# Two score products at a time: 64-row second products in the two halves of TensorE's rows

## The chip, the core and the metric

The kernel runs on one core of one Trainium2 chip. The metric is device time in microseconds (us) of one execution. All times below come from the times of three runs of the kernel before and from one profiled execution of it.

## The reference, cut to what matters

One transformer block on 2048 tokens of width 1024, in float32. Its input projection feeds two kinds of attention, and a gated convolutional feed-forward layer (1024 to 2 x 2816 and back) follows. Two of the score products matter here.

```python
# dense ("a"): 4 heads, each with 2 components c of 64 features; softmax per component, then a difference
logits = jnp.einsum('bthcd,bshcd->bhcts', qb, k).astype(jnp.float32) * scale
...
p = jax.nn.softmax(logits, axis=-1)
attn = p[:, :, 0] - lam * p[:, :, 1]
return jnp.einsum('bhts,bshe->bthe', attn.astype(v.dtype), v)

# selection: 8 index heads of 64 features against one shared key; the 256 best keys of each query stay
s_h = jax.nn.relu(jnp.einsum('bthd,bsd->bths', iqb, ik).astype(jnp.float32))
score = jnp.einsum('bth,bths->bts', iwb.astype(jnp.float32), s_h)
score = jnp.where(causal[None], score, -jnp.inf)
_, idx = lax.top_k(score, topk)
```

The sparse attention ("b", 8 heads) then works on the selected keys alone. Both attentions are causal, over 16 blocks of 128 queries.

## The kernel before

**Split operands.** Every float32 operand of a large product is kept as a float16 pair, a high part and a low part, and a product is the sum of three: high by high, high by low, low by high. A query or key of 64 features fills only half of TensorE's 128 rows, so the two halves hold different parts. In the dense logits a component's query is held twice (both halves the same, a tile of high parts and a tile of low parts), and its key has the high part in one half and the low part in the other: component 0 has its high part in rows 0 to 63, component 1 in rows 64 to 127. One product of the query's high part over 128 rows (L962) gives two of the three terms, and a second one of its low part (L963) gives the third and, unasked for, low by low. In the selection it is the query that has high and low parts in the two halves (even heads high in rows 0 to 63, odd heads in rows 64 to 127), and the key is held twice, as a tile of high parts (L1042) and one of low parts (L1043).

**The dense unit.** `a_units` yields one `a_unit` for each of 4 heads and 16 query blocks, so 64 in all. Block i has n = 128 (i + 1) keys, in chunks of up to 512. Stage `s1` goes through component 0 and then component 1: for each chunk two matmuls into a PSUM bank of tag "s", and `logits`, in which VectorE moves the chunk to the SBUF tile `big`, adds the bias near the diagonal and takes a maximum (L905, L908, L910). After the last chunk of a component come a tiny VectorE operation on the maxima (L967) and ScalarE's Exp over all n keys with a running sum (L968). Stage `s2` begins with a reciprocal of the second sum (L973), joins the two components (L977), splits the result and issues transposing DMAs (`pT`). Stage `s3` multiplies with the values (L989, L990). `pipeline` runs `s3` of one unit, `s2` of the next and `s1` of the one after side by side.

**The selection.** `att_i` takes two query blocks at a time. For each chunk of 512 keys and each of 8 heads it makes two matmuls into a bank of tag "si"; for head 0 VectorE takes the bank at once (L1046), for the other seven ScalarE makes the ReLU (L1050) and VectorE adds it to the score (L1051). Then a bitwise search for the threshold follows, 31 rounds of counting (L1073 on VectorE, L1089 on ScalarE).

**Banks.** `PSB` gives PSUM's eight banks: during the first two blocks `mm` 2, `tp` 1, `s` 2, `si` 2, `o` 1, later `mm` 2, `s` 3, `si` 2, `o` 1. The sparse units and some transposes use "s" too.

**Order.** Every engine works through its instructions in the order in which the program emits them. `timeline` picks that order: each part (selection I, dense A, sparse B and C, feed-forward F and O) is a generator that yields its own estimate of time, and the part whose due time is earliest goes on to its next yield. So between two yields of the selection or the dense logits, matmuls of the output projection or the feed-forward layer (`acc3`, L402 to L404) are usually placed. The yields of the two loops that change are

```python
yield (c1 - c0) / 960 + 0.15        # dense logits, per component and chunk
yield (c1 - c0) / 960 + 0.1         # selection, per head and chunk
```

Of the kernel before, what the change touches and what calls it, by code (L numbers as in the profile page):

```python
# [22 lines left out]
P = 128  # L23
# [58 lines left out]
def block_kernel(ctx: ExitStack, tc, x, c, w_ada, b_ada, g_attn, w_in, q_norm_a, k_norm_a, q_norm_b, k_norm_b,  # L82
# [3 lines left out]
    V, S, G, PE = nc.vector, nc.scalar, nc.gpsimd, nc.tensor  # L86
# [23 lines left out]
    def stiny(name, n=1, dt=F32):  # L110
        return small.tile([P, n], dt, name=name)
# [294 lines left out]
    def split(hi, lo, src, scale):  # L406

        S.activation(hi, src, AF.Copy, scale=scale)  # L408
        V.scalar_tensor_tensor(lo, src, scale, hi, op0=ALU.mult, op1=ALU.subtract)  # L409
# [451 lines left out]
    def chunks(n):  # L861
        out_, c0 = [], 0
        while c0 < n:
            out_.append((c0, min(n, c0 + 512)))
            c0 += 512
        return out_

    def s_ps(w, tag="s"):
        return psum.tile([P, 512], F32, name=tag, tag=tag, bufs=PSB[tag])[:, :w]
# [3 lines left out]
    def big(n):  # L873

        w = 512 if n <= 512 else 1024 if n <= 1024 else T
        at = part["at"] if part.get("w") == w else XW
        if at == XW:
            part.update(w=w, at=0, tile=X.tile([P, XW], F32, name="big", tag="big", bufs=BUFS["big"]))
            at = 0
        part["at"] = at + w  # L880
        return part["tile"][:, at:at + w]
# [9 lines left out]
    def q_tile(name, src, tag="q"):  # L891
        q = X.tile([P, 8 if tag == "qi" else 4, P], F16, name=name, tag=tag, bufs=BUFS[tag])
        n = src.shape[1] // P
        nc.sync.dma_start(q[:, 0:n].rearrange("p h q -> p (h q)"), src)
        return q

    def logits(ps, l, c0, c1, n, near, far, mx, nm):

        f = min(c1, max(c0, n - 256))
        for a0, a1 in ((c0, f), (f, c1)):  # L900
            if a1 <= a0:
                continue
            src, acc = ps[:, a0 - c0:a1 - c0], mx[:, nm:nm + 1]
            if a0 >= n - 256:
                V.tensor_tensor_reduce(l[:, a0:a1], src, near[:, 256 - (n - a0):256 - (n - a1)], 1.0, -3e38,  # L905
                                       op0=ALU.add, op1=ALU.max, accum_out=acc)
            elif far is None:
                V.tensor_scalar(l[:, a0:a1], src, 1.0, None, op0=ALU.mult, op1=ALU.max, accum_out=acc)  # L908
            else:
                V.tensor_tensor_reduce(l[:, a0:a1], src, far[:, a0:a1], 1.0, -3e38, op0=ALU.add, op1=ALU.max,  # L910
                                       accum_out=acc)
            nm += 1
        return nm
# [15 lines left out]
    def weights_v(d, pv):  # L929

        for t_ in d["pT"]:
            pv(*t_)
            yield 0.1
# [13 lines left out]
    def a_unit(t, h, i, first, ks, vs, nb, out_, os_):  # L947
        n = (i + 1) * P
        d = {}

        def s1():
            qt = q_tile("qa", qa_s[i][:, h * 512:(h + 1) * 512])
            d["L"], d["sum"] = [], stiny("a_sum", 2)
            for cc in range(2):
                l = big(n)
                d["L"].append(l)
                mx = stiny("a_mx", 5)
                nm = 0
                for c0, c1 in chunks(n):
                    ps = s_ps(c1 - c0)  # L960
                    rhs = ks[c0 // 512][:, 0:(c1 - c0) // P, cc * P:(cc + 1) * P]
                    PE.matmul(ps, qt[:, 2 * cc], rhs, start=True, stop=False)  # L962
                    PE.matmul(ps, qt[:, 2 * cc + 1], rhs, start=False, stop=True)  # L963
                    nm = logits(ps, l, c0, c1, n, nb, None, mx, nm)
                    yield (c1 - c0) / 960 + 0.15
                m = stiny("a_m")
                V.tensor_scalar(mx[:, :nm], mx[:, :nm], ga_neg, None, op0=ALU.mult, op1=ALU.min, accum_out=m)  # L967
                S.activation(l[:, :n], l[:, :n], AF.Exp, scale=ga_inv, bias=m, accum_out=d["sum"][:, cc:cc + 1])  # L968

        def s2():  # L970
            L, ssum = d["L"], d["sum"]
            bt = stiny("a_bt")
            V.reciprocal(bt, ssum[:, 1:2])  # L973
            V.tensor_scalar(bt, bt, ssum[:, 0:1], nlam, op0=ALU.mult, op1=ALU.mult)
            for c0 in range(0, n, 1024):
                c1 = min(n, c0 + 1024)
                V.scalar_tensor_tensor(L[0][:, c0:c1], L[1][:, c0:c1], bt, L[0][:, c0:c1], op0=ALU.mult, op1=ALU.add)  # L977
            yield n / 960
            yield from weights_t(d, i, L[0], gam)

        def s3():
            ssum = d["sum"]
            po = s_ps(512, "o")

            def pv(pp, b0, b1):
                for j in range(b0, b1):
                    v = vs[j // 4][:, j % 4]
                    hi, lo = pp[:, j - b0], pp[:, b1 - 2 * b0 + j]
                    PE.matmul(po[:, 0:256], hi, v, start=(j == 0), stop=False)  # L989
                    PE.matmul(po[:, 0:128], lo, v[:, 0:128], start=False, stop=(j == i))  # L990

            yield from weights_v(d, pv)
            o = X.tile([P, 2, P], F32, name="oa", bufs=2)
            S.activation(o[:, 1], po[:, 128:256], AF.Copy)
            V.tensor_tensor(o[:, 0], po[:, 0:128], o[:, 1], op=ALU.add)
            ss = stiny("a_ss", 4)
            S.activation(o[:, 1], o[:, 0], AF.Square, accum_out=ss[:, 0:1])
            V.tensor_scalar(ss[:, 1:2], ssum[:, 0:1], ssum[:, 0:1], eps_o, op0=ALU.mult, op1=ALU.mult)
            V.scalar_tensor_tensor(ss[:, 2:3], ss[:, 0:1], 1.0 / 128, ss[:, 1:2], op0=ALU.mult, op1=ALU.add)  # L999
            G.tensor_tensor(ss[:, 3:4], ss[:, 2:3], mhalf[:, 0:1], op=ALU.pow)  # L1000
            V.tensor_scalar(out_, o[:, 0], ss[:, 3:4], None, op0=ALU.mult)

        def s4():
            n_ = i - first + 1
            pt = s_ps(n_ * P)
            for j in range(n_):
                PE.transpose(pt[:, j * P:(j + 1) * P], os_[:, j], idf)
            ot = X.tile([P, 2, 2, P], F16, name="ota", bufs=1)
            pt = pt.rearrange("p (b q) -> p b q", q=P)
            split(ot[:, :, 0], ot[:, :, 1], pt, sub_c)  # L1010
            nc.sync.dma_start(ot_s[t][:, h, first % 4:first % 4 + n_], ot)
            yield 0.5

        return [s1(), s2(), s3()] if first is None else [s1(), s2(), s3(), s4()]
# [3 lines left out]
    def att_i(b0, nb_):  # L1018

        t = b0 // 4  # L1020
        for b1 in range(max(b0, 2), b0 + nb_, 2):
# [8 lines left out]
            for c in range(t + 1):  # L1030
                ki = X.tile([P, 4, 256], F16, name="ki", bufs=BUFS["ki"])
                nc.sync.dma_start(ki, ki_s[c])
                for j, i in enumerate(blks):
                    n = (i + 1) * P
                    sc_, qi = scs[j], qis[j]
                    c0, c1 = c * 512, min(c * 512 + 512, n)
                    if c1 <= c0:
                        continue
                    kk = ki[:, 0:(c1 - c0) // P]
                    for h in range(8):  # L1040
                        ps = s_ps(c1 - c0, "si")
                        PE.matmul(ps, qi[:, h], kk[:, :, 0:P], start=True, stop=False)  # L1042
                        PE.matmul(ps, qi[:, h], kk[:, :, P:2 * P], start=False, stop=True)  # L1043
                        w = iw_all[:, i, h:h + 1]
                        if h == 0:
                            V.tensor_scalar(sc_[:, c0:c1], ps, 0.0, w, op0=ALU.max, op1=ALU.mult)  # L1046
                        else:
                            nr += 1
                            r = rl[:, nr % 2, :c1 - c0]
                            S.activation(r, ps, AF.Relu)  # L1050
                            V.scalar_tensor_tensor(sc_[:, c0:c1], r, w, sc_[:, c0:c1], op0=ALU.mult,  # L1051
                                                   op1=ALU.add)
                        yield (c1 - c0) / 960 + 0.1
                    if c1 == n:
                        V.tensor_tensor(sc_[:, n - P:n], sc_[:, n - P:n], cmask, op=ALU.add)
                    V.tensor_copy(mks[j][:, c0:c1], sc_.bitcast(BF16).rearrange("p (n t) -> p n t", t=2)[:, c0:c1, 1])
# [57 lines left out]
            for j, i in enumerate(blks):  # L1114
                n = ns[j]
# [250 lines left out]
    with tc.tile_pool(name="early", bufs=1) as pool:  # L1366
        with tc.tile_pool(name="psum1", bufs=1, space=PSUM) as psum, tc.tile_pool(name="early2", bufs=1) as pool2:
# [40 lines left out]
            rs = rest()  # L1408
# [81 lines left out]
```

## Time and profile before

| | |
|---|---|
| time, median of 3 runs | 3229.09 us (3227.54 to 3232.38) |
| time of the profiled execution | 3229.96 us |
| its span, first to last instruction | 3228.3 us |
| busy: TensorE (PE) | 2823.8 us, 87% |
| busy: VectorE (DVE) | 2543.7 us, 79% |
| busy: ScalarE (ACT) | 2008.1 us, 62% |
| busy: GpSimd (POOL) | 1227.3 us, 38% |
| mean granted TensorE clock | 0.951 of full speed |

The profile has a line for each instruction: when it started and how long it is put down for. PE is a matmul, PEld the load of its weights. Matmuls overlap in the pipeline, so the step from one start to the next says what a matmul costs in a dense stretch, not its duration. A wait is the idle time of an engine just ahead of an instruction, with the work that ended it.

### The profile page before, as it was taken

Reading aid. Unit: us, or ns where it says so; the run is one execution under the profiler, and the core shown is the slowest. Engines: PE = TensorE matmul, PEld = TensorE weight load, DVE = VectorE, ACT = ScalarE, POOL = GpSimd, SP = SyncE. Lnnn points to the kernel's source line nnn. Section 1 sums busy time; section 2 is a strip of 40 time slices with the busy share of each in tenths; the row PEclk is TensorE's granted clock in tenths of the full one; section 3 lists DMA queues with packets and bytes.
Section 4 is the critical chain, followed back from the end, with each engine's and each line's share of the span. In section 5 each row is a group of like instructions: output and inputs, shape, how many; then the busy total and the mean of one; then the engine's idle time right before and its main releaser. Section 6 shows DMA issues by size and latency. Waiting matters only on the chain. (4 is left out here: it accounts for less than half of the span.)

```text
span 3228.3 us, 53238 instructions
## 1 busy us (share of the span) xinstructions
PE 2823.8 (87%) x17571; PEld 1624.0 (50%) x17571; DVE 2543.7 (79%) x6659; ACT 2008.1 (62%) x3645; POOL 1227.3 (38%) x1493
## 2 busy tenths in 40 slices
PE   5799896986899898978898999789899898888899
PEld 3345453543666475644444544444444445656476
DVE  8766888887988999977999898796788967977222
ACT  5977654563755675778555975567746678556133
POOL 2100354220656275502650660006516602845155
PEclk9999897998899899989999999889999998999899
DMA  9798875426887779996458879964685598799776
GB/s 352 240 361 301 300 274 178 142 62 217 209 233 221 196 213 235 250 275 170 118 156 236 184 185 268 256 188 122 184 240 146 139 297 220 220 245 240 222 226 202
DMA packets 741142, 704.02 MB, mean 218 GB/s; under 512 B 474362, under 2 KB 583166, under 8 KB 739584
## 3 DMA queue, kind: packets, MB, share of 16 engines
q1 hardware_dynamic: 740864, 700.61, 76.5%
q8 instruction: 138, 2.26, 0.3%
q14 instruction: 140, 1.15, 0.1%
HBM read 483.24 MB, written 114.21 MB: 185 GB/s over the span
## 5 line engine op out<-in xcount | busy, mean ns | idle before, releaser
L402 PE MATMUL mm<-h2T,wu 128*128 128x256 f16 (+1 forms) x2112 | 656.2, 311 | 34.9 <-ACT ua L1287 22.0
L404 PE MATMUL mm<-h2T,wu 128*128 128x256 f16 (+1 forms) x2112 | 656.8, 311 | 0.0
L403 PE MATMUL mm<-h2T,wu 128*128 128x256 f16 (+1 forms) x2112 | 656.8, 311 | 0.0
L1089 ACT ACTIVATE cjunk<-sc,sel 128x512 bf16<-128x512 f32 (+10 forms) x281 | 395.7, 1408 | 170.1 <-DVE cjunk L1073 140.6
L1290 POOL TENSOR_SCALAR u<-ut,cws 128x256 f32<-128x256 f32 (+1 forms) x264 | 363.1, 1375 | 294.6 <-ACT ut L1285 286.7
L402 PE MATMUL mm<-wd,gT 128*128 128x512 f16 x704 | 272.1, 387 | 35.9 <-DMA wd<-wd_s 15.6
L1291 POOL TENSOR_TENSOR ua<-ua,u 128x256 f32<-128x256 f32 (+1 forms) x264 | 271.6, 1029 | 78.3 <-DVE ua L1288 60.1
L403 PEld LDWEIGHTS <-wu 128*128 128x128 f16 x2112 | 208.7, 99 | 134.0 <-issue 32.6
L403 PE MATMUL mm<-wd,gT 128*128 128x512 f16 x704 | 271.7, 386 | 0.0
L404 PE MATMUL mm<-wd,gT 128*128 128x512 f16 x704 | 271.6, 386 | 0.0
L402 PEld LDWEIGHTS <-wu 128*128 128x128 f16 x2112 | 209.0, 99 | 114.9 <-DMA wu<-wu_s 11.4
L404 PEld LDWEIGHTS <-wu 128*128 128x128 f16 x2112 | 208.9, 99 | 107.2 <-issue 1.7
L402 PE MATMUL mm<-wg,hT 128*128 128x512 f16 (+1 forms) x640 | 242.4, 379 | 16.4 <-DVE kn L487 9.6
L1288 DVE SCALAR_TENSOR_TENSOR ua<-ut,cws,ua 128x256 f32<-128x256 f32 (+1 forms) x264 | 168.4, 638 | 103.8 <-ACT ua L1287 98.5
L403 PE MATMUL mm<-wg,hT 128*128 128x512 f16 (+1 forms) x640 | 242.3, 379 | 3.5 <-DVE wg L371 3.5
L481 POOL TENSOR_TENSOR hn_r<-hn_t,mhalf 128x8 f32<-128x8 f32 (+1 forms) x64 | 97.9, 1533 | 379.2 <-DVE hn_t L479 293.9
L1000 POOL TENSOR_TENSOR a_ss<-a_ss,mhalf 128x1 f32<-128x1 f32 x64 | 46.8, 732 | 506.9 <-DVE a_ss L999 274.7
L404 PE MATMUL mm<-wg,hT 128*128 128x512 f16 (+1 forms) x640 | 236.0, 377 | 2.4 <-DVE hT L396 2.4
L1051 DVE SCALAR_TENSOR_TENSOR sc<-relu,iw_all,sc 128x512 f32<-128x512 f32 (+3 forms) x266 | 214.1, 805 | 22.0 <-ACT relu L1050 17.9
L1173 ACT ACTIVATE big<-big,b_m,gb_inv 128x128 f32<-128x128 f32 (+15 forms) x128 | 165.2, 1291 | 77.6 <-DVE b_mx L1172 77.0
L1050 ACT ACTIVATE relu<-si 128x512 f32<-128x512 f32 (+3 forms) x266 | 139.7, 538 | 116.3 <-PE si L1043 76.8
L409 DVE SCALAR_TENSOR_TENSOR hl<-big,hl 128x1024 f16<-128x1024 f32 (+7 forms) x192 | 186.8, 984 | 31.5 <-ACT hl L408 30.7
(338 smaller groups left out, 7322.1 us busy)
## 6 DMA issues: line engine op xcount, KB each, us to landing
wu<-wu_s SPq DMA_DIRECT2D x264, 512.0 KB, 4.8
wd<-wd_s SPq DMA_DIRECT2D x160, 512.0 KB, 4.8
wo<-wo_s SPq DMA_DIRECT2D x64, 512.0 KB, 5.0
wst<-in_w_ada_dram SPq DMA_DIRECT2D x22, 1024.0 KB, 10.2
wst<-in_w_up_dram SPq DMA_DIRECT2D x22, 1024.0 KB, 11.8
wu_s<-wp SPq DMA_DIRECT2D x22, 1024.0 KB, 6.4
xd<-x_s SPq DMA_DIRECT2D x64, 256.0 KB, 6.4
ka<-ka_s SPq DMA_DIRECT2D x60, 256.0 KB, 5.7
```

Of the source, the lines that this page charges most:

```text
L402: PE.matmul(ps, a(0, k), b(0, k), start=(first and k == k0), stop=False)
L403: PE.matmul(ps, a(0, k), b(1, k), start=False, stop=False)
L404: PE.matmul(ps, a(1, k), b(0, k), start=False, stop=(last and k == k0 + nk - 1))
L409: V.scalar_tensor_tensor(lo, src, scale, hi, op0=ALU.mult, op1=ALU.subtract)
L481: G.tensor_tensor(r[:, :nh], t[:, :nh], mhalf[:, :nh], op=ALU.pow)
L1050: S.activation(r, ps, AF.Relu)
L1051: V.scalar_tensor_tensor(sc_[:, c0:c1], r, w, sc_[:, c0:c1], op0=ALU.mult, op1=ALU.add)
L1089: S.activation(junk[:, :ns[j]], scs[j][:, :ns[j]], AF.Sign, bias=C[:, j:j + 1].bitcast(F32), accum_out=cnt[:, j:j + 1])
L1173: S.activation(l[:, :n], l[:, :n], AF.Exp, scale=gb_inv, bias=m[:, 0:1], accum_out=m[:, 1:2])
L1288: V.scalar_tensor_tensor(a, ut[:, 1:n + 1], cws[:, 1, cc:cc + 1], a, op0=ALU.mult, op1=ALU.add)
L1290: G.tensor_scalar(u0, ut[:, 0:n], cws[:, 0, cc:cc + 1], None, op0=ALU.mult)
L1291: G.tensor_tensor(a, a, u0, op=ALU.add)
```

## The change

The heads of the selection and the components of the dense logits are taken in pairs. Both first products of a pair come first, each over 128 rows into a bank of its own. Then come both second products, each over the 64 rows that hold the wanted term: rows 0 to 63 for one, rows 64 to 127 for the other. The low by low term is no longer computed. The number of matmuls, of yields and of evictions stays. Two further things move. Both banks of a pair are taken at its start; and in the dense unit the loop over chunks is now the outer one, so the two small maxima operations and the two Exps of a unit stand together behind the last chunk, where the first component's used to stand ahead of the second component's chunks.

```diff
             d["L"], d["sum"] = [], stiny("a_sum", 2)
+            mxs, nms = [], [0, 0]
             for cc in range(2):
-                l = big(n)
-                d["L"].append(l)
-                mx = stiny("a_mx", 5)
-                nm = 0
-                for c0, c1 in chunks(n):
-                    ps = s_ps(c1 - c0)
-                    rhs = ks[c0 // 512][:, 0:(c1 - c0) // P, cc * P:(cc + 1) * P]
-                    PE.matmul(ps, qt[:, 2 * cc], rhs, start=True, stop=False)
-                    PE.matmul(ps, qt[:, 2 * cc + 1], rhs, start=False, stop=True)
-                    nm = logits(ps, l, c0, c1, n, nb, None, mx, nm)
+                d["L"].append(big(n))
+                mxs.append(stiny("a_mx", 5))
+            for c0, c1 in chunks(n):
+                pss = [s_ps(c1 - c0), s_ps(c1 - c0)]
+                kc = ks[c0 // 512][:, 0:(c1 - c0) // P]
+                for cc in range(2):
+                    PE.matmul(pss[cc], qt[:, 2 * cc], kc[:, :, cc * P:(cc + 1) * P], start=True, stop=False)
+                for cc in range(2):
+                    rs = slice(64 * cc, 64 * cc + 64)
+                    PE.matmul(pss[cc], qt[rs, 2 * cc + 1], kc[rs, :, cc * P:(cc + 1) * P], start=False, stop=True)
+                for cc in range(2):
+                    nms[cc] = logits(pss[cc], d["L"][cc], c0, c1, n, nb, None, mxs[cc], nms[cc])
                     yield (c1 - c0) / 960 + 0.15
+            for cc in range(2):
+                l, mx, nm = d["L"][cc], mxs[cc], nms[cc]
                 m = stiny("a_m")
                 V.tensor_scalar(mx[:, :nm], mx[:, :nm], ga_neg, None, op0=ALU.mult, op1=ALU.min, accum_out=m)
                 S.activation(l[:, :n], l[:, :n], AF.Exp, scale=ga_inv, bias=m, accum_out=d["sum"][:, cc:cc + 1])
...
                     kk = ki[:, 0:(c1 - c0) // P]
+                    pss = []
                     for h in range(8):
-                        ps = s_ps(c1 - c0, "si")
-                        PE.matmul(ps, qi[:, h], kk[:, :, 0:P], start=True, stop=False)
-                        PE.matmul(ps, qi[:, h], kk[:, :, P:2 * P], start=False, stop=True)
+                        if h % 2 == 0:
+                            pss = [s_ps(c1 - c0, "si"), s_ps(c1 - c0, "si")]
+                            for e in range(2):
+                                PE.matmul(pss[e], qi[:, h + e], kk[:, :, 0:P], start=True, stop=False)
+                            for e in range(2):
+                                rs = slice(64 * e, 64 * e + 64)
+                                PE.matmul(pss[e], qi[rs, h + e], kk[rs, :, P:2 * P], start=False, stop=True)
+                        ps = pss[h % 2]
```

## Rows read from the trace of the kernel before

**Rows 1.** Page, busy time of each engine and its share of the span.
```profile
PE 2823.8 (87%) x17571; PEld 1624.0 (50%) x17571; DVE 2543.7 (79%) x6659; ACT 2008.1 (62%) x3645; POOL 1227.3 (38%) x1493
```

**Rows 2.** Stretches with selection or dense logits: length, busy of each engine, clock, DMA.
```profile
1540.00:1700.00 160.00, 145.88 (x774) 72.35 (x773) 154.05 (x325) 89.06 (x162) 94.25 (x85) 1.00 0.52 146
2360.00:2500.00 140.00, 135.66 (x824) 68.15 (x823) 116.03 (x232) 81.06 (x132) 61.57 (x61) 1.00 0.75 191
```

**Rows 3.** Groups by line and shape, the second products: count, busy, mean ns, idle.
```profile
L963 PE MATMUL s<-ka,qa 128*128 128x512 f16 x224 | 90.9, 406 | 0.0
L1043 PE MATMUL si<-ki,qi 128*128 128x512 f16 x224 | 86.3, 385 | 0.0
L963 PE MATMUL s<-ka,qa 128*128 128x384 f16 x32 | 11.2, 350 | 0.0
L1043 PE MATMUL si<-ki,qi 128*128 128x384 f16 x32 | 10.4, 326 | 0.0
L963 PE MATMUL s<-ka,qa 128*128 128x256 f16 x32 | 8.7, 273 | 0.0
L963 PE MATMUL s<-ka,qa 128*128 128x128 f16 x32 | 7.2, 228 | 0.0
L1043 PE MATMUL si<-ki,qi 128*128 128x256 f16 x24 | 7.1, 301 | 0.0
L1043 PE MATMUL si<-ki,qi 128*128 128x128 f16 x24 | 5.1, 219 | 0.0
```

**Rows 4.** Timeline of PE near 1066 us: start, duration, what.
```profile
1065.97 0.33 PE L963 MATMUL s<-ka,qa 128*128 128x384 f16 x1
1066.13 0.38 PE L962 MATMUL s<-ka,qa 128*128 128x512 f16 x1
1066.35 0.38 PE L963 MATMUL s<-ka,qa 128*128 128x512 f16 x1
...
1067.26 0.28 PE L989 MATMUL o<-va,pT 128*128 128x256 f16 x1 [0.21 <-DMA pT<-hl]
1067.38 0.22 PE L990 MATMUL o<-va,pT 128*128 128x128 f16 x1
1067.43 0.27 PE L989 MATMUL o<-va,pT 128*128 128x256 f16 x1
1067.54 0.22 PE L990 MATMUL o<-va,pT 128*128 128x128 f16 x1
```

**Rows 5.** Timelines of PEld and PE around a 32-row product near 128 us; its line.
```profile
127.77 0.31 PEld L404 LDWEIGHTS <-hT 128*128 128x128 f16 x2
128.51 0.10 PEld L760 LDWEIGHTS pb<-b_tmp,b_rb 32*12 32x12 f32 x2 [0.42 <-issue]
129.25 0.10 PEld L402 LDWEIGHTS <-hT 128*128 128x128 f16 x1 [0.64 <-issue]
...
127.99 0.59 PE L404 MATMUL mm<-wg,hT 128*128 128x512 f16 x2
128.51 0.81 PE L760 MATMUL pb<-b_tmp,b_rb 32*12 32x384 f32 x2
129.25 0.39 PE L402 MATMUL mm<-wg,hT 128*128 128x512 f16 x1
129.48 0.38 PE L403 MATMUL mm<-wg,hT 128*128 128x512 f16 x1
...
L760 PE MATMUL pb<-b_tmp,b_rb x2: 481/484/488, 128.5 to 128.8; 32*12 32x384 f32 x2
```

**Rows 6.** Waits, whole span: who for whom, us in total, times, longest.
```profile
PE si L1042 <- ACT relu L1050: 17.3, 20, 2.1
PE si L1042 <- DVE sc L1046: 4.7, 8, 1.6
...
DVE a_bt L973 <- ACT big L968: 6.1, 8, 1.9
...
ACT big L968 <- DVE a_mx L967: 72.7, 55, 11.2
```

**Rows 7.** The line of the dense Exp, durations ns min/median/max; the ReLU by shape.
```profile
L968 ACT ACTIVATE big<-big,a_m,ga_inv x128: 478/1289/2114, 571.1 to 2815.1; 128x128 f32<-128x128 f32 x8, 128x256 f32<-128x256 f32 x8, 128x384 f32<-128x384 f32 x8, 128x512 f32<-128x512 f32 x8
L968 ACT ACTIVATION_READ_ACCUMULATOR big<-big,a_m,ga_inv x128: 183/187/223, 571.5 to 2817.1; 128x1 f32 x128
...
L1050 ACT ACTIVATE relu<-si 128x512 f32<-128x512 f32 x196 | 113.6, 592 | 103.0 <-PE si L1043 68.9 <-DVE sc L1051 17.9 <-DVE mask L1120 10.9
```

## The prediction

> **What bounds the kernel now.** I read the page's busy shares first. TensorE is busy 87% of the span and VectorE 79% [rows 1], so both can be the bound, each in its own stretches, and a saving on TensorE counts in full only where VectorE has room. Next come stretches in which the edited loops run. From 2360 to 2500 us TensorE is busy 135.66 of 140 us and VectorE 116.03: there the end follows TensorE. From 1540 to 1700 us VectorE is busy 154.05 of 160 us and TensorE 145.88: there TensorE time is mostly covered [rows 2]. Both run at a granted clock of 1.00, the 2.4 GHz level. The edited loops lie in stretches of either kind, so I let a change of TensorE's time move the end by half of itself. That factor is my choice; the ends of it are 0 (second stretch) and 1 (first).
>
> Then I read what the products cost (the groups by line and shape, and a timeline), what happens around a product with few rows (timelines of the two TensorE rows), and the waits of the engines at the edited lines.
>
> **What the change could take away on TensorE.** The second products number 224 + 32 + 32 + 32 in the dense logits and 224 + 32 + 24 + 24 in the selection, by widths of 512, 384, 256 and 128 columns [rows 3]. In pairs that is 160 + 152 = 312 pairs: 224 of 512 columns, 32 of 384, 28 of 256, 28 of 128. Each line shows no idle time ahead of it, so these matmuls follow the one before at once. What one costs is the step to the next start, not its duration: 0.22 us for 512 columns (1066.13 to 1066.35), 0.16 for 384 (1065.97 to 1066.13), 0.11 for 256 and 0.05 for 128 (1067.38, .43, .54) [rows 4]. I use 0.216, 0.160, 0.108 and 0.056, which fit those steps and lie in proportion. If the two second products of a pair run wholly at the same time, one step per pair goes: 224 x 0.216 + 32 x 0.160 + 28 x 0.108 + 28 x 0.056 = 48.4 + 5.1 + 3.0 + 1.6 = 58.1 us. If they run one after the other, nothing goes. No row shows two products in different rows at one time, so 58.1 and 0 are both ends. I take 58.1, because the rows of the next step show that TensorE does treat a product of few rows apart from a full one.
>
> **What the change adds on TensorE.** Each pair now goes from 128-row work to 64-row work and back. The nearest row is the one product in the trace over 32 rows (L760). Ahead of it the second L404 starts at 127.99 + 0.59 - 0.38 = 128.20 and has its columns in by 128.42; the 32-row matmul starts at 128.51, 0.09 late. Its weights, too, start at 128.51, while ordinary weights start together with the matmul ahead of their own. Behind it, the second of the pair starts at 128.51 + 0.81 - 0.48 = 128.84 and by the step of the two (0.33) is in at 129.17; the next 128-row weights and matmul start only at 129.25, 0.08 late, and the step after that is 0.23 instead of 0.22 [rows 5]. Together about 0.19 us for going there and back. It is float32 with 12 weight columns, so it is near, not equal. The ends are 0 (rows 0 to 63 and 64 to 127 need no such change-over) and 0.19; with nothing nearer I take 0.19, so 312 x 0.19 = 59.3 us. The second half-product's weights cost little more: behind a wait for `pT` a weight load and its matmul lose 0.12 - 0.11 = 0.01 us [rows 4], so 312 x 0.01 = 3 us.
>
> The Trainium skill, "TensorEngine Tiling (Array Packing)", section Tiling Modes, Key Properties, says that going over to another tiling mode, as against another tile of the same mode, drains TensorE; that speaks against a change that goes over twice for one saved step. It gives no price; the trace agrees with it at the one place where it can, by the 0.19 us above. Without that rule the sum would be the 58.1 us saved, with it the near break-even of the next sentence.
>
> TensorE's sum is -58.1 + 59.3 + 3 = about +4 us, so it does not matter much that only half of it counts: +2. A 512-column pair gains 0.216 - 0.20 = 0.016 us, a 128-column pair loses 0.14.
>
> **What moves: the Exps.** In the dense unit the first Exp now stands just ahead of the second. ScalarE gets nothing more to do, but the reciprocal that opens `s2` on VectorE (L973) waits for the second sum, and all of VectorE's later work is queued behind it: evictions, on which TensorE's banks hang, and the joined row, on which the `pT` transposes hang. An Exp and its sum take 1.29 + 0.19 = 1.48 us at the median [rows 7]. Upper end: 64 x 1.48 = 95 us of VectorE waiting; lower end 0. ScalarE sits idle ahead of 55 of 128 Exps [rows 6], and only there does a later start make a later end (elsewhere the other work behind it has moved forward by as much): 64 x 0.43 x 1.48 = 41 us. L973 waits only 8 times now, 6.1 us in all [rows 6], so most units have some slack; I leave half, 20 us, and let a third of that reach the end, since VectorE is the bound only in part of the stretches and gives way to the `pT` chain in a few others: +7 us.
>
> **What moves: the banks.** The selection has two "si" banks. Before, TensorE filled one while ScalarE emptied the other; now a pair takes both, and its second first-product waits for the odd head of the pair before. TensorE waits at L1042 28 times now, 17.3 + 4.7 us [rows 6]. There the wait can grow by one ReLU of 0.59 us [rows 7]: 28 x 0.59 = 17 us at most, 0 at least where feed-forward matmuls lie between. These waits lie largely where VectorE or ScalarE is late anyway, so I count a quarter: +4 us. The dense logits have three "s" banks and keep one in hand; nothing for them, up to the same 17 us if VectorE is late there. The two maxima operations, the evictions, the DMA issues and the yields are as many as before: nothing.
>
> **The sum.** +2 + 7 + 4 = +13 us on the profiled execution's 3229.96 us (its span is 3228.3), so 3243. That execution is 0.9 us above the median of the runs, so I say 3242 us, 0.4% slower. A measurement of this kernel tells about 0.2%, 6.5 us, from no change.
>
> **The rivals.**
>
> Going over is free (faster). One mechanism: TensorE passes from 128 rows to the half rows with no gap, the weights being loaded ahead as usual. Then -58 + 3 = -55 us on TensorE, half of it -28, +11 for Exps and banks: 3213 us. Counted in full it would be 3185. For it: L760 differs in type and in weight columns as well as in rows, so its 0.19 need not be the rows' [rows 5]. Against it: those two gaps are all the trace has. It decides once the going over costs less than about 0.09 us a pair.
>
> No overlap (much slower). The half-products run one after the other, and the going over is paid: +59 + 3 = +62 us on TensorE, half of it +31, +11: 3271 us. For it: no row shows overlap. Against it: nothing in the rows either.
>
> The banks and Exps alone decide. TensorE comes out even and the moved work is hidden (VectorE's waits fall in stretches that TensorE bounds): 3232 us, no change that can be told. Then feed-forward matmuls between the yields cover everything [rows 2].
>
> The Trainium skill, "TensorE: Matmul & The Clock Gate", Part 3, gives the rule for the overlap of the first sum: matmuls in different row groups start some 4 ns apart; no run here shows it yet.
>
> **How the numbers follow.** Break-even on TensorE with the moved work showing: 0.40, 3242 us (3235 to 3256 of its own). Moved work hidden: 0.12, 3232 us. Going over free: 0.30, 3213 us (3185 to 3226). No overlap: 0.18, 3271 us (3255 to 3295). The range leaves out a tenth at each end: the lower third of the free case and the upper half of the last one, 3198 to 3278. Faster by over 0.2%: 0.26 of the free case and 0.05 of the others, 0.31. Within: 0.03 + 0.09 + 0.08 = 0.20. Slower: the rest, 0.49.
>
> **What would show it.** Starts of the half-products: the pair's two starts nearly together and the next matmul one step behind them (overlap), or a step apart. The gap ahead of the first half-product and behind the second: 0.09 us each, with weights that start late, if I am right; none in the free case. The wait of L973 for the Exp should grow from 6.1 us to some 20 to 30, and the waits of the selection's first products from 22 us to some 30 to 40. Half-products that need much more than 0.1 us at each end, or clock falls around them, would make me wrong on the slow side; starts in the usual steps of 0.22 with 0.43 us fewer for every two pairs on the fast side.

## The result, and the profile after

The changed kernel takes 3267.31 us (median of 4 runs, 3258.0 to 3273.42), against 3228.56 us for the kernel before on the same chip: a ratio of 1.0115, 95% interval 1.0086 to 1.0144. It is 1.15% slower. The forecast was 3242 us, within 3198 to 3278.

The page of the profile after, its span and busy times, answers to [rows 1]:

```profile
span 3271.7 us, 53150 instructions
PE 2922.3 (89%) x17556; PEld 1592.9 (49%) x17571; DVE 2544.0 (78%) x6659; ACT 2010.4 (61%) x3645; POOL 1221.7 (37%) x1493
```

TensorE is busy 2922.3 - 2823.8 = 98.5 us more, the other engines as before. Its idle time (span minus busy) went from 404.5 to 349.4 us. So, between these two executions, 55 of the 98.5 us went into time in which TensorE used to wait, and 43 lengthened the span. My sum had +4 us of TensorE time.

The same two stretches as in [rows 2], each line with length, busy time of PE, PEld, DVE, ACT, POOL, clock, DMA:

```profile
1540.00:1700.00 160.00, 151.67 (x734) 64.29 (x732) 145.89 (x314) 97.21 (x169) 103.21 (x92) 0.98 0.49 129
2360.00:2500.00 140.00, 132.11 (x694) 58.94 (x693) 110.59 (x205) 63.30 (x101) 38.82 (x40) 0.94 0.79 199
```

In the first, VectorE was the fuller engine (154.05 against 145.88) and now TensorE is (151.67 against 145.89). TensorE issues 734 matmuls in these 160 us instead of 774, and is busier. (The stretch does not hold quite the same work as before, since all that comes ahead of it takes longer.) In the second, the granted clock fell from 1.00 to 0.94.

The waits that I named, after (VectorE, ScalarE and TensorE rows of the whole span, to set beside [rows 6]):

```profile
DVE a_bt L978 <- ACT big L973: 11.7, 12, 2.6
ACT big L973 <- DVE a_mx L972: 35.9, 27, 5.6
PE si L1050 <- ACT relu L1061: 5.8, 7, 1.8
PE si L1050 <- DVE sc L1057: 1.7, 2, 1.5
```

The reciprocal waits 11.7 us instead of 6.1, not the 20 to 30 forecast, and the selection's first products wait 7.5 us instead of 22.0, not 30 to 40. ScalarE's wait for the maxima has halved (72.7 before). Of the two things that I had put on the moved work the first happened in small part, the second not at all. The reason for the loss is in the timelines. Here is PE and then PEld at one place: start, duration, what.

```profile
1594.22 0.38 PE L404 MATMUL mm<-h2T,wu 128*128 128x512 f16 x1
1594.43 0.38 PE L962 MATMUL s<-ka,qa 128*128 128x512 f16 x1
1594.75 0.39 PE L965 MATMUL s<-ka,qa 64*128 64x512 f16 x1
1595.07 0.39 PE L402 MATMUL mm<-h2T,wu 128*128 128x512 f16 x1
1595.29 0.38 PE L403 MATMUL mm<-h2T,wu 128*128 128x512 f16 x1
...
1594.22 0.10 PEld L962 LDWEIGHTS <-qa 128*128 128x128 f16 x1
1594.74 0.09 PEld L965 LDWEIGHTS <-qa 64*128 64x128 f16 x1 [0.42 <-issue]
1595.06 0.10 PEld L402 LDWEIGHTS <-wu 128*128 128x128 f16 x1 [0.23 <-issue]
```

The way to 64 rows costs 0.32 - 0.22 = 0.10 us ahead of the half-product (L965) and another 0.10 us behind it, and both times the weights start only with their own matmul, where ordinary weights start with the matmul ahead (L962 at 1594.22). That is the price read from L760 [rows 5]. The Trainium skill, "TensorEngine Tiling (Array Packing)", section Tiling Modes, Key Properties, has the rule that a change of mode drains TensorE; this trace agrees, and puts 0.20 us on going there and back.

But the half-product stands alone. Its partner is elsewhere, with its own first product. A few us later:

```profile
1598.58 0.38 PE L962 MATMUL s<-ka,qa 128*128 128x512 f16 x1 [1.62 <-DVE big L908]
1598.89 0.39 PE L965 MATMUL s<-ka,qa 64*128 64x512 f16 x1
1599.21 0.39 PE L404 MATMUL mm<-h2T,wu 128*128 128x512 f16 x1
1599.44 0.38 PE L962 MATMUL s<-ka,qa 128*128 128x512 f16 x1
1599.75 0.39 PE L965 MATMUL s<-ka,qa 64*128 64x512 f16 x1
1600.07 0.39 PE L402 MATMUL mm<-h2T,wu 128*128 128x512 f16 x1
```

The first product waited 1.62 us for VectorE to empty its bank. Its half-product, a feed-forward matmul and only then another first product follow. The program emits two first products and then two second ones; the instructions of an engine are not issued in that order. As I read it, a planner at compile time (`schedule_with_timeline_sim=True` in the last lines of the kernel) puts first what its own simulation has ready, and with few banks the partner's bank is often not free; no run isolates that reason. My account of the kernel before said that each engine works in the order of emission. That is wrong, and the trace of the kernel before shows it. A first product of the dense logits (L962) and its second (L963) are emitted one directly behind the other, and yet:

```profile
1598.25 0.38 PE L962 MATMUL s<-ka,qa 128*128 128x512 f16 x1
1598.46 0.38 PE L1042 MATMUL si<-ki,qi 128*128 128x512 f16 x1
1598.68 0.38 PE L1043 MATMUL si<-ki,qi 128*128 128x512 f16 x1
1598.89 0.38 PE L963 MATMUL s<-ka,qa 128*128 128x512 f16 x1
```

Counted along the timeline of PE, the half-products of the dense logits stand alone 202 times and next to another 59 times (202 + 2 x 59 = 320), those of the selection 282 and 11 times (282 + 2 x 11 = 304). So 70 of 312 pairs are next to each other. Where they are, the change does what it says:

```profile
1563.26 0.59 PE L962 MATMUL s<-ka,qa 128*128 128x512 f16 x2
1563.79 0.39 PE L965 MATMUL s<-ka,qa 64*128 64x512 f16 x2
1564.11 0.39 PE L402 MATMUL mm<-h2T,wu 128*128 128x512 f16 x1
```

Two half-products together (x2) are put down for 0.39 us, as one is, and the next matmul starts 0.32 us behind them, as behind one. The Trainium skill, "TensorE: Matmul & The Clock Gate", Part 3, has matmuls in different row groups start about 4 ns apart; these rows, which resolve 0.01 us, agree.

With 0.20 us for each of 484 lone half-products, and about nothing for the 70 pairs (0.20 us paid, up to 0.22 saved), TensorE's sum is about +97 us, an estimate from these counts and steps. The busy times show +98.5.

### The profile page after: what moved, and what is told of

Its sections match the earlier page's. It is cut to its first block, busy times and chain, and to the rows that moved or that the text cites. A ratio compares the mean times of both kernels' runs of the same rounds, so it can differ in the third digit from the quotient of the medians.

```text
span 3271.7 us, 53150 instructions
## 1 busy us (share of the span) xinstructions
PE 2922.3 (89%) x17556; PEld 1592.9 (49%) x17571; DVE 2544.0 (78%) x6659; ACT 2010.4 (61%) x3645; POOL 1221.7 (37%) x1493
## 3 DMA queue, kind: packets, MB, share of 16 engines
q14 instruction: 140, 1.15, 0.1%
## 4 chain that ended last, share of the span: by engine, by line
PE 41%; DVE 24%; DMA 10%; ACT 9%; issue 9%; POOL 2%; SPq 1%; DVEq 0%; ACTq 0%; POOLq 0%
PE mm L402 10%; PE mm L403 10%; PE mm L404 10%; ACT cjunk L1100 4%; DVE cjunk L1084 4%; DMA pT<-hl 3%; DVE hl L409 2%; PE si L1053 2%; DMA xt<-in_x_dram 2%; PE si L1050 1%; DVE big L908 1%; PE o L994 1%; PE s L965 1%; PE s L962 1%; PE o L1198 1%
## 5 line engine op out<-in xcount | busy, mean ns | idle before, releaser
L1301 POOL TENSOR_SCALAR u<-ut,cws 128x256 f32<-128x256 f32 (+1 forms) x264 | 349.7, 1325 | 341.7 <-ACT ut L1296 292.8
L1302 POOL TENSOR_TENSOR ua<-ua,u 128x256 f32<-128x256 f32 (+1 forms) x264 | 280.5, 1063 | 64.8 <-DVE ua L1299 46.2
L1062 DVE SCALAR_TENSOR_TENSOR sc<-relu,iw_all,sc 128x512 f32<-128x512 f32 (+3 forms) x266 | 205.0, 771 | 43.3 <-ACT relu L1061 40.5
```

What stands on the lines that cost most here:

```text
L1301: G.tensor_scalar(u0, ut[:, 0:n], cws[:, 0, cc:cc + 1], None, op0=ALU.mult)
L1302: G.tensor_tensor(a, a, u0, op=ALU.add)
```

## The experiments

All ratios are against the kernel before, run on the same chip, with 95% intervals. The first four runs were made to separate three things: the rows, the order, and the moved Exps and banks.

**Pairs kept together.** Ordering edges (issue order only, no wait for a result) chain the four matmuls of a pair:

```diff
+    def after_(bi, prev):
+        tc.add_manual_dep(bi.ins, prev.ins.name,
+                          mybir.DependencyInfo(mybir.DependencyClass.NoSync, mybir.DependencyReason.DATA), reason="order")
+        return bi
...
-                    PE.matmul(pss[cc], qt[rs, 2 * cc + 1], kc[rs, :, cc * P:(cc + 1) * P], start=False, stop=True)
+                    last = after_(PE.matmul(pss[cc], qt[rs, 2 * cc + 1], kc[rs, :, cc * P:(cc + 1) * P], start=False,
+                                            stop=True), last)
```

> The changed kernel, with ordering edges that keep each pair's four matmuls in their order, so that the two half-products stand next to each other (307 of 312 pairs; in the changed kernel 70). Theory O (the order split the pairs, and every lone half-product pays the way to 64 rows and back, 0.20 us, with no partner to overlap with): PE busy falls back by some 95 us from 2922, the time to 3225 to 3242. Theory M (the moved Exps and the banks taken in pairs cost the time, the half rows are neutral): stays at 3255 to 3275. Theory W (keeping pairs together makes TensorE wait for the second bank): PE busy falls, but waits ahead of the first products grow by over 40 us and the time stays above 3250.

Measured: 3261.07 us, 1.0125 (1.0108 to 1.0142). PE busy fell to 2847.7 us as theory O has it, and the time did not follow. As it stands this refutes O as an account of the whole: with the lone half-products gone, the kernel is still as slow. What theory W named is there, in TensorE's waits at the first products:

```profile
PE s L969 <- DVE big L914: 31.8, 28, 4.1
PE s L969 <- DVE a_mx L911: 13.8, 15, 2.1
PE s L969 <- DVE ota L415: 4.2, 3, 1.8
PE si L1060 <- ACT relu L1073: 21.1, 24, 2.0
PE si L1060 <- DVE sc L1069: 6.8, 9, 1.8
```

These are 77.7 us, against 13.5 + 10.8 + 2.2 + 5.8 + 1.7 = 34.0 at the same places of the changed kernel. But the edges may also have changed the order in other ways, and the waits do not tell the two apart.

**All 128 rows.** The changed kernel with its second products as before:

```diff
-                    PE.matmul(pss[cc], qt[rs, 2 * cc + 1], kc[rs, :, cc * P:(cc + 1) * P], start=False, stop=True)
+                    PE.matmul(pss[cc], qt[:, 2 * cc + 1], kc[:, :, cc * P:(cc + 1) * P], start=False, stop=True)
...
-                                PE.matmul(pss[e], qi[rs, h + e], kk[rs, :, P:2 * P], start=False, stop=True)
+                                PE.matmul(pss[e], qi[:, h + e], kk[:, :, P:2 * P], start=False, stop=True)
```

> The changed kernel, order and all, but its second products over all 128 rows as before. Theory O: the loss goes, 3222 to 3240; what is left over the kernel before is the price of the moved Exps and banks, forecast at 11 us. Theory M: the loss stays, 3255 to 3275.

Measured: 3217.96 us, 0.9983 (0.9970 to 0.9996). The loss is gone, and slightly more: theory M falls. This is the one version that is faster than both kernels, by 0.17% against the kernel before, and hardly clear of nothing.

**Half rows in the loops of before.** One product at a time, the second over its 64 rows:

```diff
-                    PE.matmul(ps, qt[:, 2 * cc + 1], rhs, start=False, stop=True)
+                    rs = slice(64 * cc, 64 * cc + 64)
+                    PE.matmul(ps, qt[rs, 2 * cc + 1], ks[c0 // 512][rs, 0:(c1 - c0) // P, cc * P:(cc + 1) * P],
+                              start=False, stop=True)
...
-                        PE.matmul(ps, qi[:, h], kk[:, :, P:2 * P], start=False, stop=True)
+                        rs = slice(64 * (h % 2), 64 * (h % 2) + 64)
+                        PE.matmul(ps, qi[rs, h], kk[rs, :, P:2 * P], start=False, stop=True)
```

> The kernel before, its loops and order kept, with only the second products cut to their 64 rows: 624 lone half-products. Theory O: 624 x 0.20 = 125 us more PE time than before, PE busy near 2950, and at the rate at which the change turned 98 us of PE busy into 39 us of time, 3270 to 3290. Theory M: 3225 to 3235.

Measured: 3271.54 us, 1.0154 (1.0133 to 1.0175), PE busy 2941.1 us. As theory O expects.

**Pairs together, all 128 rows.** The first experiment with the rows of the second:

> The kernel of e1_together with second products over all 128 rows: pairs kept in order, no half rows. Theory O: a 512-column pair saves 0.216 and pays 0.20, narrower ones lose, so this is within 0.3% of e1_together. If overlap of the halves were worth more than the way there and back, e1_together would be faster than this by over 10 us; if the way cost more, slower by over 10 us. Theory W: this is slow as well, above 3250.

Measured: 3239.7 us, 1.0069 (1.0044 to 1.0093), below the 3250 of theory W. By the ratios the first experiment was 18 us slower than this one, more than the 10 us I allowed for break-even. But each of these kernels has its own order: the traces of the changed kernel and of the second experiment, which differ in the rows alone, show other sequences on TensorE, VectorE, ScalarE and GpSimd. A difference of 18 us between two such kernels need not be the rows.

So the next four were made with the order pinned. The kernel traces its program twice. The first trace gives the planner's order for one row count; the second has the other row count and ordering edges between neighbours of that order, on every engine. The two then issue the same instructions in the same order, and differ only in the rows.

```diff
+            traced = {i.name: i for i in nc.cur_bb.bb.instructions}
+            for names in (order or {}).values():
+                names = [n for n in names if n in traced]
+                for p, n in zip(names, names[1:]):
+                    tc.add_manual_dep(traced[n], p, mybir.DependencyInfo(mybir.DependencyClass.NoSync,
+                                                                         mybir.DependencyReason.DATA), reason="order")
...
-                    rs = slice(64 * cc, 64 * cc + 64)
+                    rs = slice(64 * cc, 64 * cc + 64) if HALF else slice(0, P)
```

**The order of the changed kernel, all 128 rows.**

> Every engine's instructions in exactly the order of the changed kernel, only the second products over all 128 rows. Theory R (the half rows themselves cost the time, mostly as 484 lone half-products at 0.20 us): the loss goes, 0.995 to 1.003 of the kernel before. Theory Q (the order that the planner makes around half rows is what is slow): 1.007 to 1.013, as the changed kernel. With the changed kernel's 1.0115 this splits the change into order and rows exactly.

Measured: 3224.45 us, 0.9998 (0.9985 to 1.0010), PE busy 2827.4 us. The order of the changed kernel, with its moved Exps and its banks taken in pairs, costs nothing that can be told. All of the 1.15% is the half rows. Busy time against the changed kernel: 2922.3 - 2827.4 = 95 us, for 3271.7 - 3224.6 = 47 us of span.

**The order of before, half rows.**

> Every engine's instructions in exactly the order of the kernel before, only the second products cut to their 64 rows, 624 of them, each alone. Theory R: 624 x 0.205 = 128 us more PE time, of which 35 to 50 us reach the end: 1.011 to 1.016. Theory Q: 1.000 to 1.005, the loss of e3_halves_alone having come from its other order.

Measured: 3269.9 us, 1.0138 (1.0114 to 1.0162), PE busy 2943.3 us, 119.5 more than before: 0.19 us for each of the 624. Its PE timeline shows the way there and back time after time, each with both gaps:

```profile
1594.35 0.38 PE L963 MATMUL s<-ka,qa 128*128 128x512 f16 x1
1594.66 0.39 PE L965 MATMUL s<-ka,qa 64*128 64x512 f16 x1
1594.98 0.39 PE L963 MATMUL s<-ka,qa 128*128 128x512 f16 x1
1595.30 0.39 PE L965 MATMUL s<-ka,qa 64*128 64x512 f16 x1
```

**Pairs together, the order pinned, half rows.**

> Every engine's instructions in exactly the order of e4_together_full (pairs together), with the second products cut to their 64 rows. Theory S (only steps count: a pair pays 0.205 us for the way and saves the step of one matmul, 312 x 0.205 - 58.1 = +6 us of PE): within 0.3% of e4_together_full's 1.0069. Theory C (half rows also leave TensorE at the 1.2 GHz level for longer, as the three half-row traces with 199 to 221 us there against 168 to 192 in the three full-row ones suggest): 1.010 to 1.014, with a lower granted clock in the stretches of dense logits. Theory Q: as S, e1_together's 1.0125 having come from its other order.

Measured: 3250.9 us, 1.0078 (1.0063 to 1.0093), PE busy 2837.0 us against 2838.4 in the same order with 128 rows, whose ratio is 1.0069 (1.0044 to 1.0093). Theory S holds: to within the 0.3% that these ratios tell, a pair that stands together neither gains nor loses. This run and the first experiment have the same instructions and differ in their order alone, 1.0078 against 1.0125: most of the 18 us was order.

Theory C, that half rows lower the clock, had the time at 1.010 to 1.014, and it is below. The clock itself does not dismiss it. The mean granted clock is 0.950 in both profiled executions, but over all runs it is 0.947 to 0.950 with half rows and 0.950 to 0.958 with full rows, and likewise 0.946 to 0.949 in the changed kernel against 0.949 to 0.954 in its order with full rows. So in these pairs of kernels half rows go with slightly more time at the 1.2 GHz level. What that costs was not separated; the gaps alone, 97 us, leave little of TensorE's added 95 us for it.

**Both half-products in rows 0 to 63.** For one of each pair these are the wrong rows, so its result is another sum.

```diff
-                    rs = slice(64 * cc, 64 * cc + 64) if HALF else slice(0, P)
+                    rs = slice(0, 64) if HALF else slice(0, P)
```

> As e6_together_pinned, but both half-products of a pair take rows 0 to 63 (so the second of each pair computes with the wrong half of its operands). If the two overlap because they stand in different rows, here they must follow each other: starts 0.22 us apart, no gap between them, the gaps of 0.10 us only ahead of the first and behind the second; 58 us more PE time than e6_together_pinned, PE busy up by about that much, and 15 to 30 us more in all. If they overlap whatever their rows are, as e6_together_pinned.

Measured: 3264.65 us, 1.0120 (1.0103 to 1.0137), PE busy 2895.7 us, 58.7 more than with different halves, where 58 were expected; 14 us more time, where 15 to 30 were. The same pair in the two PE timelines, first with different halves and then, from the other kernel, with the same half:

```profile
1594.15 0.38 PE L970 MATMUL s<-ka,qa 128*128 128x512 f16 x1
1594.46 0.39 PE L974 MATMUL s<-ka,qa 64*128 64x512 f16 x2
1594.78 0.33 PE L1022 MATMUL s<-idf,oas 128*128 128x128 f32 x1
```

```profile
1595.19 0.38 PE L970 MATMUL s<-ka,qa 128*128 128x512 f16 x1
1595.51 0.60 PE L974 MATMUL s<-ka,qa 64*128 64x512 f16 x2
1596.04 0.33 PE L1022 MATMUL s<-idf,oas 128*128 128x128 f32 x1
```

The pair takes 0.39 us in different halves, so both start at once, and 0.60 in the same half, so they start 0.21 apart. The next matmul follows 0.32 behind the first of the one pair and 0.53 behind the first of the other: one step more, but no second gap of 0.10. The price is for the way, not for each half-product. And the overlap needs different halves.

**Four together.** If two are break-even, four should gain. Against the kernel with pairs together, the selection takes four heads at a time and the dense logits two chunks of both components (not shown); the banks of tags "s" and "si" are put together:

```diff
-                        if h % 2 == 0:
-                            pss = [s_ps(c1 - c0, "si"), s_ps(c1 - c0, "si")]
+                        if h % nh == 0:
+                            pss = [s_ps(c1 - c0, "si") for _ in range(nh)]
...
-    PSB = dict(mm=2, s=3, si=2, o=1)
+    PSB = dict(mm=2, s=5, o=1)
```

> One way there and back for four half-products instead of two, wherever there are four: the banks of tags s and si are put together (four, later five), the selection takes four heads at a time, the dense logits two chunks of both components; ordering edges keep a group's products together (179 groups for the 624 half-products). Theory S: a group of four pays 0.205 us and saves two steps of 0.216, so PE busy is some 58 - 179 x 0.205 = 21 us below that of e10_fours_full in the same order, and the time 8 to 15 us below it. Holding four products together should cost at least what holding two did (0.7%), so against the kernel before 1.003 to 1.020. If the way there and back were paid by each half-product and not by each group, PE busy would be above that of e10_fours_full.

> Every engine's instructions in exactly the order of e9_fours, with second products over all 128 rows. Theory S: 8 to 15 us slower than e9_fours; against the kernel before 1.006 to 1.024, all of it from holding four products together.

Measured: 3405.92 us, 1.0542 (1.0521 to 1.0563), and with 128 rows in the same order 3401.94 us, 1.0526 (1.0501 to 1.0552). A group of four takes two steps and one way:

```profile
1749.45 0.38 PE L972 MATMUL s<-ka,qa 128*128 128x512 f16 x1
1749.76 0.60 PE L977 MATMUL s<-ka,qa 64*128 64x512 f16 x4
1750.30 0.39 PE L410 MATMUL mm<-h2T,wu 128*128 128x512 f16 x1
```

The first of the four starts 0.31 behind the product ahead, and the next matmul follows 0.54 behind it: one more step of 0.22, then the same 0.32. PE busy is 2843.3 us against 2853.7, so 10 us are saved where 21 were expected. The 8 to 15 us of time that I expected from it are not there: the half rows come out 4 us slower, within the noise. TensorE is busy only 84% of the span here and idle for 560 us of it. Taking four products at a time, with the banks put together, costs 5%, where I had put 0.3 to 2%; the two were not separated, and the granted clock is lower too (0.927 in the profiled execution, 0.951 before). Two long waits carry a part of that (the longest at the selection's first products was 13.0 us before):

```profile
PE si L1064 <- DVE sc L1073: 44.4, 2, 43.9
PE si L1064 <- DMA ki<-ki_s: 40.7, 1, 40.7
```

## Why the prediction was right in sign and low in size

**Going there and back, 0.19 us (right).** Read off one place with 32-row products in float32 (0.09 ahead, 0.08 and 0.01 behind, which make 0.18 and not the 0.19 that I wrote), it holds for 64-row products in float16: 0.10 ahead and 0.10 behind, weights late both times.

**Overlap of the halves, one step saved for each pair (right where it can happen).** Both start at once in different halves, and a step apart in the same one.

**The sum on TensorE, -58.1 + 59.3 + 3 = +4 us (the step that failed).** It counted 312 ways and 312 saved steps, because it took the two half-products of a pair to be neighbours. They are in 70 of 312 pairs. The other 242 pairs go there and back twice and save nothing: 484 x 0.20 = 97 us. With pairs held together and the order pinned, the sum is near the forecast (PE busy -1.4 us against +4).

**Half of TensorE's time reaches the end (somewhat high).** From the pinned kernel to the changed one it is 47 of 95 us by the spans of the profiled executions but, by the ratios 0.9998 and 1.0115, 38 of 95. With lone halves in the order of before it is 0.0138 x 3227 = 45 of 119.5 us, and for both half-products in the same rows 14 of 58.7. So it is a quarter to two fifths.

**The moved Exps +7 us, the banks +4 us (wrong, both are nothing).** The changed order with full rows is at 0.9998 (0.9985 to 1.0010). The wait of the reciprocal did grow, by 5.6 us where I had 14 to 24, and the time does not show it. The selection's waits shrank.

So the time lies in the range, and the direction is right, but not by the case I held likeliest, and that it lies in the range is luck: the range reached up to 3278 only because of halves that do not overlap. The wrong steps worked against each other: 93 us too little on TensorE, against 11 us too much for the moved work and a share that was too high. With the share from the order of before (45 of 119.5), 97 us make 37 us; 39 were measured. Of the rivals, "no overlap" with 3271 us comes nearest to the time and is not what happens: the halves overlap whenever they meet. What I had missed was a rival of its own, that the change does not do what it says for most pairs. The trace of the kernel before could have told: its lines near 1598 us, shown above, have other work between two products that are emitted as neighbours.

What stays open: why holding pairs together costs 0.7% (fourth experiment against the pinned order of the change). TensorE's waits at the first products are not enough to show it: its idle time (span minus busy) grows from 397 to 414 us, spread over many lines, and the profiled execution of the fourth experiment (3254.49 us) is one of the two slowest of six. Open too is what the lower granted clock of the half-row kernels costs.

## What to carry to other kernels

Before a change that needs two instructions to be neighbours, look in the trace whether the planner keeps neighbours together, and count them afterwards. Two half-row products of 512 columns side by side save just what the way to half rows and back costs (0.22 against 0.20 us), so the trick needs more than two in a row. Four saved TensorE 10 us here, but no run turned that into time: what it took to have four side by side cost 5%. To compare two versions of an operation, pin the order of one on the other: here it turned a puzzling 18 us into 3, which is within the noise.

## What the runs showed of the hardware that I had not expected

The way to fewer rows is paid by the visit, not by the instruction: three kernels with 0.31 or 0.32 us ahead, and 0.32 behind the half-product that starts last, whether one, two or four half-products stand in between. And at the one place that shows it, the way from 128 to 32 rows in float32 costs about the same as the way from 128 to 64 rows in float16 (0.18 and 0.20 us).
